# Hybrid encoder trunk on one core: more lead for the filter on VectorE, outer gates of convolution A behind the attention inputs, per-tile staging of the first chunks, five single tiles ahead of doubles in layer 1

## The chip, the cores and the metric

The program runs on one core of a Trainium2 chip. The metric is device time in microseconds (us).

## What is computed

Two layers over a sequence of 2048 positions with 1024 channels, then a final RMSNorm. Cut to what matters:

```
h = rmsnorm(x, norm_g);  proj = h @ w_in           # 1024 -> 3584, 28 tiles of 128 channels
y_a = silu(layernorm(depthwise_conv31(a_u * sigmoid(a_v)) + b)) * silu(a_z)
y_b = b_b * conv3(b_c * b_x) * silu(b_z)
y_c = window_attention(c_q, c_k, c_v, sink) * silu(c_z)      # +-128 positions
y_d = neighbourhood_attention(d_q, d_k, d_v, rpb) * silu(d_z)
x = x + concat(y_a, y_b, y_c, y_d) @ w_out         # 1024 -> 1024, 8 tiles of 128
```

## The kernel before

**Tiles and stages.** The sequence is cut into four chunks of 512 positions. Every fp32 operand of a projection is split in two (hi and lo), and three products are added, so one weight tile of 128 channels on one chunk is 24 matmuls of 512 columns. A job (run, line 859) takes one weight tile over one chunk (a single) or over two chunks (a double, 48 matmuls). The stages are, in order: i00 and i01 (input projection of layer 0, chunks 0 and 1, then 2 and 3), o00 (output projection, chunks 0 and 1), i10, o01, i11, o10, o11. The chunks of a pair sit in slots s0 and s1; an output stage reads its chunk's Y back from DRAM into the same slots (place_y_steps, line 329). In an input stage (in_jobs, line 896) the first RU = 3 tiles run as singles on the first chunk and then on the second, the last RD = 3 likewise, and those between are doubles.

**Weights.** Each half of a weight tile is loaded by SyncE's DMA queue (load_w), cast by ScalarE to whi and subtracted by VectorE to wlo (split_w, line 849). The next job's second half is split after the 24th matmul of a single, twelve matmuls before it is needed.

**The other work.** Attention goes in units (line 628) of 128 queries and two heads: scores s, a softmax on VectorE and ScalarE, transposes pt, products o, and a gate ag; 32 units for each chunk pair, 16 for one chunk, 64 in a layer. They begin once their inputs are marked done (marks, lines 923 and 926). The 31 taps of the depthwise convolution are 31 VectorE instructions for each of two channel tiles and each chunk (tap_steps, line 465). When both channel tiles of a chunk have their taps and the gates az are stored, conv_ln (line 490) runs the LayerNorm and writes Y; it uses POOL for sums, PE for lnm, lnv and rb, and the same two PSUM buffers "s" as the units' scores. Output chunk c waits for its 16 units and for the LayerNorms of chunks c and c+1 (y_ready, line 975).

**What sets the order.** The Python code is a planner that writes out the program order. After every eight matmuls it calls point (line 180), which advances evictions, units and background work and then adds taps. It keeps two clocks of its own: PE by a cost for each matmul (0.228 for one of 512 columns), DVE by 0.12 + 0.00115 per element, never below PE's clock less 1:

```
                clk["dve"] = max(clk["dve"], clk["pe"] - 1.0) + 0.12 + n * 1.15e-3
        while taps and clk["dve"] < clk["pe"] + LEAD:
            tap()
```

These are planning numbers and no times. When built, the framework's scheduler takes the program order as priority and lets an instruction go earlier on its engine where its inputs and buffers are free by its own estimate. In ev_au (line 447) taps are forced out when four filters are queued, and before an odd output chunk of layer 1 the planner waits until no taps are left (line 963). GA = 4 buffers hold gated inputs (gA) and four hold filter sums (accA); TB = 5 buffers "t" serve gates, squares and the LayerNorm.

**The first chunks.** scale_steps multiplies all eight tiles of a chunk by the norm, and then place_steps splits them (lines 296 and 318); chunk 1 goes the same way in second (line 1072). bias_steps (line 761) copies a table for the relative bias into DRAM 128 times (rep, 2256 KB), loads it back and writes the bias tiles; it is called once for each layer.

Of the kernel before, what the change touches and what calls it, by code (L numbers as in the profile page):

```python
# [18 lines left out]
P = 128  # L19
# [36 lines left out]
TB, TH, XTB, GA, GB = 5, 2, 4, 4, 4  # L56
QSB, PRB, PTB = 2, 4, 2
GRP = 8
RU, RD = 3, 3
PF, UNITS, SPACING = 7, 4, 5  # L60
PF_LATE, UNITS_LATE, SPACING_LATE = 3, 6, 2
LEAD = 0.0
KSB, VTB, WB = 3, 3, 3

E_A_U, E_A_V, E_A_Z = 0, 2, 4
# [6 lines left out]
def trunk(ctx, tc, xT, w_in, w_out, par, sink, rpb, fg, trig, cmask, dmask, out):  # L72
# [16 lines left out]
    def T(pool_, shape, dt, tag, bufs, name=None):  # L89
        uid[0] += 1  # L90
        return pool_.tile(shape, dt, tag=tag, bufs=bufs, name=f"{name or tag}_{uid[0]}")
# [78 lines left out]
    evs, bg, units, taps = [], [], [], deque()  # L170
    waiting, done = [], set()
    current, gap, points, begun, turn = [None], [0], [0], [0], [0, 0]
    pace = {"spacing": SPACING, "units": UNITS, "pf": PF}

    def advance(lst):
        for g in list(lst):
# [3 lines left out]
    def point():  # L180
        advance(evs)
        advance(units)
        gap[0] += 1
        points[0] += 1
        if waiting and gap[0] >= pace["spacing"] and len(units) < pace["units"] and begun[0] < turn[0] + QSB:
            group = current[0] or next((w for w in waiting if w[0]()), None)
            if group:
                current[0] = group
                gap[0] = 0
                g = group[1].popleft()()  # L190
                if not group[1]:
                    waiting.remove(group)
                    current[0] = None
                units.append(g)
                next(g)
        advance(bg)
        while taps and clk["dve"] < clk["pe"] + LEAD:
            tap()

    def tap():  # L200
# [24 lines left out]
    def new_slot(s):  # L225
        return (pairs(slot, F32R, f"s{s}h", 4), pairs(slot, F32R, f"s{s}l", 4))
# [25 lines left out]
    def spread(r, n):  # L252
        rb = T(ps, [P, CH], F32, "s", 2, "rb")
        for b in range(0, n, P):
            m = min(P, n - b)
            mm(rb[:, b:b + m], r[:m, b // P:b // P + 1].broadcast_to([m, P]), ident[:m, :m], True, True, 0.12)
        return rb
# [38 lines left out]
    def scale_steps(l, c, xts, per=2):  # L296
        rb = spread(RC[l][:, 4 * c:4 * c + 4], CH)
        yield
        rs = T(gp, [P, CH], F32, "t", TB, "rs")
        act.copy(out=rs, in_=rb)  # L300
        yield
        for k in range(KT):
            dve.scalar_tensor_tensor(out=xts[k], in0=xts[k], scalar=LP[l]["par"][:, PG + k:PG + k + 1], in1=rs,
                                     op0=ALU.mult, op1=ALU.mult)
            if k % per == per - 1:
                yield
        staged[(l, c)] = xts

    def stage_steps(l, c):
        while ("rc", l, c) not in done:  # L310
# [7 lines left out]
    def place_steps(l, c, s):  # L318
        while (l, c) not in staged:
            yield  # L320
        xts = staged.pop((l, c))
        hi, lo = new_slot(s)
        for k in range(KT):
            split(xts[k], hi[k], lo[k])
            if k % 2:
                yield
        acts[(l, c)] = (hi, lo)
# [433 lines left out]
    def bias_steps(l):  # L761
        L = LP[l]
        W = 4 * RPR * RPW
        sp.dma_start(out=L["rep"], in_=rpb[l:l + 1, :].broadcast_to([P, W]))
        yield from hold(4)
        n = 15 * RPW + 32
        Ms = []
        for h in range(4):
            M = T(ap_, [P, 2 * CH], F32, "ks", KSB, "bm") if h < 3 else T(ap_, [P, 2 * CH], F32, "vt", VTB, "bm")
            base = L["rep"][0:1, :]  # L770
            src = bass.AP(tensor=base.tensor, offset=base.offset + h * RPR * RPW + 7 * RPW + 15,
                          ap=[[16 * W - RPW, 8], [W - 1, 16], [1, n]])
            sp.dma_start(out=M[:, :n], in_=src)
            Ms.append(M[:, :16 * RPW].rearrange("p (r c) -> p r c", c=RPW))
        for (o, sz, i, j) in MOFF.values():
            R, rr, C = window(i, j)
            mk = T(ap_, [P, CH], F32, "pth", PTB, "bmk")
            sp.dma_start(out=mk[:, :sz], in_=dmask[:, o:o + sz])
            r0, c0 = ROW_M0[i], COL_M0[j]
            mkv = mk[:, :sz].rearrange("p (g r c) -> p g r c", r=rr, c=C)  # L780
            yield
            yield
            for p in range(2):
                t = T(ap_, [P, 2, CH], F32, "prob", PRB, "bmo")
                for hh in range(2):
                    pool.tensor_tensor(out=t[:, hh, :sz].rearrange("p (g r c) -> p g r c", r=rr, c=C), in0=mkv,  # L786
                                       in1=Ms[2 * p + hh][:, r0:r0 + R, c0:c0 + C].rearrange(
                                           "p (r g) c -> p g r c", r=rr), op=ALU.subtract)
                yield from hold(2)
                sp.dma_start(out=L["bias"][2 * p:2 * p + 2, :, o:o + sz].rearrange("h q n -> q h n"), in_=t[:, :, :sz])  # L790
        done.add(("bias", l))
# [104 lines left out]
    def in_jobs(l, half):  # L896
        A, B = ((0, 1), (2, 3))[half]
        D = [(E_D_K, lambda p: lambda c, pt: ev_dk(l, p, c, pt)),
             (E_D_V, lambda p: lambda c, pt: ev_vd(l, p, c, pt)),
             (E_D_Q, lambda p: lambda c, pt: ev_dq(l, p, c, pt)),  # L900
             (E_D_Z, lambda p: lambda c, pt: ev_z(l, 6 + p, c, pt))]
        lst = [(et + p, ev(p), None) for et, ev in D for p in range(2)]
        C = [(E_C_K, lambda c, pt: ev_rope(l, "k", 0, c, pt), lambda: [load_trig(c) for c in (A, B)]),
             (E_C_V, lambda c, pt: ev_vc(l, c, pt), None),
             (E_C_Q, lambda c, pt: ev_rope(l, "q", 0, c, pt), None),
             (E_C_Q + 1, lambda c, pt: ev_rope(l, "q", 1, c, pt), None),
             (E_C_Z, lambda c, pt: ev_z(l, 4, c, pt), None),
             (E_C_Z + 1, lambda c, pt: ev_z(l, 5, c, pt), None)]
        Aa = []
        for e in range(2):  # L910
            Aa += [(E_A_V + e, lambda c, pt, e=e: ev_av(l, e, c, pt), None),
                   (E_A_U + e, lambda c, pt, e=e: ev_au(l, e, c, pt), None)]
        for e in range(2):
            Aa.append((E_A_Z + e, lambda c, pt, e=e: ev_z(l, e, c, pt), None))
        Bb = []
        for e in range(2):
            Bb += [(E_B_C + e, lambda c, pt, e=e: ev_bc(l, e, c, pt), None),
                   (E_B_X + e, lambda c, pt, e=e: ev_bx(l, e, c, pt), None),
                   (E_B_Z + e, lambda c, pt, e=e: ev_bz(l, e, c, pt), None),
                   (E_B_B + e, lambda c, pt, e=e: ev_bb(l, e, c, pt), None)]  # L920
        if half == 0:
            order = lst + C + Aa + Bb
            marks = {7: ("qd", l, 0), 13: ("qc", l, 0), 19: [("az", l, 0), ("az", l, 1)]}
        else:
            order = Aa + lst + C + Bb
            marks = {5: [("az", l, 2), ("az", l, 3)], 13: ("qd", l, 1), 19: ("qc", l, 1)}

        def mark(i):
            ks = marks[i] if isinstance(marks[i], list) else [marks[i]]

            def late():
                yield from hold(8)
                for k in ks:
                    done.add(k)
            bg.append(late())

        N = len(order)

        def emit(i, keys, last):
            et, ev, pre = order[i]  # L940
            job(wtile(l, et), keys, ev, pre if keys[0][-1] == A or len(keys) == 2 else None,
                (lambda: mark(i)) if last and i in marks else None)

        for i in range(RU):
            emit(i, [(l, A)], False)
        for i in range(RU):
            emit(i, [(l, B)], True)
        for i in range(RU, N - RD):
            emit(i, [(l, A), (l, B)], True)
        for i in range(N - RD, N):  # L950
            emit(i, [(l, A)], False)
        first = len(jobs) - 1
        for i in range(N - RD, N):
            emit(i, [(l, B)], True)
        return first, len(jobs) - 1
# [73 lines left out]
    then(o10[1], y_place(1, 3, 1))  # L1029

    def late():
        pace.update(spacing=SPACING_LATE, units=UNITS_LATE, pf=PF_LATE)
        return
        yield

# [28 lines left out]
            pass  # L1064
    for hf in range(2):
        split_w(jobs[0], hf)
    for _ in scale_steps(0, 0, x0):
        pass
    for _ in place_steps(0, 0, 0):
        pass  # L1070

    def second():
        yield from stat_steps(1, x1)
        yield from scale_steps(0, 1, x1)
        yield from place_steps(0, 1, 1)

    def consts():
        yield from hold(3)
# [98 lines left out]
```

## Time and profile before

| | us |
|---|---|
| median of 3 runs (2089.1 to 2099.12) | 2096.69 |
| the profiled execution | 2092.12 |
| its span, first to last instruction | 2090.3 |
| PE busy in the span | 1967.2 |
| VectorE (DVE) busy | 1553.1 |
| ScalarE (ACT) busy | 1040.1 |

The profile shows one execution. Matmul ends are modelled and overlap, so PE's pace is read from starts: two starts of a steady stretch tell how long one matmul holds the engine. A window row gives busy time, granted clock (1.00 is 2.4 GHz, 0.50 is 1.2 GHz) and DMA share of a stretch.

### The profile page before, as it was taken

Reading aid. Unit: us, or ns where it says so; the run is one execution under the profiler, and the core shown is the slowest. Engines: PE = TensorE matmul, PEld = TensorE weight load, DVE = VectorE, ACT = ScalarE, POOL = GpSimd, SP = SyncE. Lnnn points to the kernel's source line nnn. Section 1 sums busy time; section 2 is a strip of 40 time slices with the busy share of each in tenths; the row PEclk is TensorE's granted clock in tenths of the full one; section 3 lists DMA queues with packets and bytes.
Section 4 is the critical chain, followed back from the end, with each engine's and each line's share of the span. In section 5 each row is a group of like instructions: output and inputs, shape, how many; then the busy total and the mean of one; then the engine's idle time right before and its main releaser. Section 6 shows DMA issues by size and latency. Waiting matters only on the chain.

```text
span 2090.3 us, 29475 instructions
## 1 busy us (share of the span) xinstructions
PE 1967.2 (94%) x9436; PEld 1638.5 (78%) x9436; DVE 1553.1 (74%) x3531; ACT 1040.1 (50%) x2217; POOL 181.6 (9%) x158
## 2 busy tenths in 40 slices
PE   5899999999999999899999999989999899996697
PEld 4778888787888878788888888878888788885585
DVE  6734799968985677776659998755995567866855
ACT  4435434523355466566654446532237566665542
POOL 0610000071010000000100000001000000100100
PEclk9999999999999999999999999999999999998698
DMA  9985533576455479867653467863638866577353
GB/s 281 305 280 175 150 121 92 170 257 200 151 172 171 158 246 305 242 201 236 183 164 119 143 179 220 244 197 105 179 132 252 227 193 207 154 221 221 120 177 115
DMA packets 233850, 400.65 MB, mean 192 GB/s; under 512 B 26848, under 2 KB 92000, under 8 KB 233440
## 3 DMA queue, kind: packets, MB, share of 16 engines
q1 hardware_dynamic: 233696, 398.77, 62.2%
q8 instruction: 75, 1.23, 0.3%
q14 instruction: 79, 0.65, 0.1%
HBM read 297.68 MB, written 105.61 MB: 193 GB/s over the span
## 4 chain that ended last, share of the span: by engine, by line
PE 71%; DMA 14%; DVE 9%; ACT 2%; issue 2%; SPq 1%; POOL 1%; DVEq 0%; POOLq 0%; ACTq 0%
PE mm L135 59%; PE o L135 3%; PE s L135 3%; PE pt L716 3%; DMA prob<-bias 2%; DMA wraw<-in_w_in_dram 2%; DVE wlo L128 1%; DMA s1l<-Y 1%; DVE xt L128 1%; DMA qs<-QD 1%; DMA qs<-QC 1%; DMA wraw<-in_w_out_dram 1%; POOL bmo L786 1%; DMA Y<-accA 1%; DVE accA L128 1%
## 5 line engine op out<-in xcount | busy, mean ns | idle before, releaser
L135 PE MATMUL mm<-s1h,whi 128*128 128x512 f32 x1152 | 458.8, 399 | 22.5 <-ACT s1h L218 10.8
L218 ACT CAST whi<-wraw 128x512 fp32r<-128x512 f32 x400 | 246.6, 618 | 444.9 <-PE mm L135 348.9
L135 PE MATMUL mm<-s1l,whi 128*128 128x512 f32 x1152 | 457.8, 398 | 6.2 <-DVE s1l L128 6.2
L135 PE MATMUL mm<-s0h,whi 128*128 128x512 f32 x1152 | 455.4, 396 | 7.0 <-ACT s0h L218 5.3
L135 PE MATMUL mm<-s0l,whi 128*128 128x512 f32 x1152 | 454.4, 395 | 4.9 <-DVE s0l L128 4.9
L135 PE MATMUL mm<-s1h,wlo 128*128 128x512 f32 x1152 | 455.2, 397 | 4.0 <-DVE wlo L128 4.0
L135 PE MATMUL mm<-s0h,wlo 128*128 128x512 f32 x1152 | 455.3, 396 | 1.0 <-DVE wlo L128 0.7
L128 DVE TENSOR_TENSOR wlo<-wraw,whi 128x512 fp32r<-128x512 f32 x400 | 289.3, 725 | 159.7 <-ACT whi L218 142.4
L128 DVE SCALAR_TENSOR_TENSOR accA<-gA,par,accA 128x512 f32<-128x512 f32 (+1 forms) x480 | 352.8, 774 | 0.6
L135 PEld LDWEIGHTS mm<-s1h,whi 128*128 128x128 f32 x1152 | 219.6, 191 | 69.8 <-ACT s1h L218 12.1
L135 PEld LDWEIGHTS mm<-s1l,whi 128*128 128x128 f32 x1152 | 219.9, 191 | 51.0 <-DVE s1l L128 7.5
L135 PEld LDWEIGHTS mm<-s0h,whi 128*128 128x128 f32 x1152 | 218.2, 190 | 51.5 <-ACT s0h L218 5.7
L135 PEld LDWEIGHTS mm<-s1h,wlo 128*128 128x128 f32 x1152 | 219.7, 191 | 49.4 <-DVE wlo L128 5.9
L135 PEld LDWEIGHTS mm<-s0l,whi 128*128 128x128 f32 x1152 | 218.2, 189 | 50.2 <-DVE s0l L128 6.3
L135 PEld LDWEIGHTS mm<-s0h,wlo 128*128 128x128 f32 x1152 | 218.2, 189 | 45.5 <-DVE wlo L128 3.2
L689 ACT ACTIVATE prob<-prob,mn 128x384 f32<-128x384 f32 (+4 forms) x256 | 155.3, 607 | 116.1 <-DVE mn L128 115.0
L706 ACT ACTIVATE prob<-prob,sm 128x384 f32<-128x384 f32 (+4 forms) x256 | 142.2, 602 | 49.8 <-DVE sm L128 43.9
L128 DVE TENSOR_TENSOR pth<-pt,pth 128x512 fp32r<-128x512 f32 (+3 forms) x248 | 138.5, 573 | 32.6 <-ACT pth L218 31.6
L135 PE MATMUL s<-ks,qs 128*128 128x384 f32 (+4 forms) x512 | 129.6, 357 | 21.1 <-DMA qs<-QC 7.0
L218 ACT CAST pth<-pt 128x512 fp32r<-128x512 f32 (+3 forms) x248 | 115.0, 495 | 66.6 <-PE pt L716 46.1
L135 PE MATMUL o<-pth,vt 128*128 128x256 f32 (+2 forms) x784 | 129.6, 297 | 8.2 <-DVE oy L128 5.2
L135 PEld LDWEIGHTS o<-pth,vt 128*128 128x128 f32 (+2 forms) x784 | 117.4, 199 | 20.7 <-issue 4.1
(120 smaller groups left out, 2039.5 us busy)
## 6 DMA issues: line engine op xcount, KB each, us to landing
wraw<-in_w_in_dram SPq DMA_DIRECT2D x272, 256.0 KB
wraw<-in_w_out_dram SPq DMA_DIRECT2D x128, 256.0 KB
qs<-QD SPq DMA_DIRECT2D x128, 128.0 KB
qs<-QC SPq DMA_DIRECT2D x128, 128.0 KB
G<-g SPq DMA_DIRECT2D x48, 256.0 KB
vt<-VD SPq DMA_DIRECT2D x144, 72.0 KB
xt<-in_xT_dram SPq DMA_DIRECT2D x20, 512.0 KB
KD<-t SPq DMA_DIRECT2D x32, 256.0 KB
```

What stands on the lines that cost most here:

```text
L128: return fn(*a, **kw)
L135: pe.matmul(out=out, lhsT=lhsT, rhs=rhs, start=start, stop=stop)
L218: act.copy(out=hi, in_=src)
L689: act.activation(out=t[:, hh, :n], in_=t[:, hh, :n], func=AF.Exp, bias=mn[:, hh:hh + 1], scale=-1.0, accum_out=sm[:, hh:hh + 1])
L706: act.activation(out=t[:, hh, :n], in_=t[:, hh, :n], func=AF.Copy, scale=sm[:, hh:hh + 1])
L716: pe.transpose(out=tp[:kw, b_, hh, :], in_=t[:, hh, kb * kw:(kb + 1) * kw], identity=ident)
L786: pool.tensor_tensor(out=t[:, hh, :sz].rearrange("p (g r c) -> p g r c", r=rr, c=C), in0=mkv, in1=Ms[2 * p + hh][:, r0:r0 + R, c0:c0 + C]. ...
```

## The change

LEAD becomes 6.0 in both layers, so taps are written out until the DVE clock is 6 ahead of PE's. In the second input stage of each layer the order was: six tiles of convolution A, attention inputs D and C, then B; now the four tiles u and v of A come first, then D and C, then the two gates az, then B; the marks follow. In layer 1 the first five tiles are singles in place of three. The first two chunks are scaled and split tile by tile. The copy rep is tied behind the DMA that was written just before it.

```diff
-RU, RD = 3, 3
+RU, RU1, RD = 3, 5, 3
-LEAD = 0.0
+LEAD, LEAD_LATE = 6.0, 6.0
...
-        while taps and clk["dve"] < clk["pe"] + LEAD:
+        while taps and clk["dve"] < clk["pe"] + pace["lead"]:
             tap()
...
+    def scale_place_steps(l, c, xts, s):
+        rb = spread(RC[l][:, 4 * c:4 * c + 4], CH)
+        yield
+        rs = T(gp, [P, CH], F32, "t", TB, "rs")
+        act.copy(out=rs, in_=rb)
+        yield
+        hi, lo = new_slot(s)
+        for k in range(KT):
+            dve.scalar_tensor_tensor(out=xts[k], in0=xts[k], scalar=LP[l]["par"][:, PG + k:PG + k + 1], in1=rs,
+                                     op0=ALU.mult, op1=ALU.mult)
+            split(xts[k], hi[k], lo[k])
+            if k % 2:
+                yield
+        acts[(l, c)] = (hi, lo)
...
-        sp.dma_start(out=L["rep"], in_=rpb[l:l + 1, :].broadcast_to([P, W]))
+        tc.keep_in_program_order(sp.dma_start(out=L["rep"], in_=rpb[l:l + 1, :].broadcast_to([P, W])))
...
-            order = Aa + lst + C + Bb
-            marks = {5: [("az", l, 2), ("az", l, 3)], 13: ("qd", l, 1), 19: ("qc", l, 1)}
+            order = Aa[:4] + lst + C + Aa[4:] + Bb
+            marks = {11: ("qd", l, 1), 17: ("qc", l, 1), 19: [("az", l, 2), ("az", l, 3)]}
...
-        for i in range(RU):
+        ru = RU1 if l else RU
+        for i in range(ru):
             emit(i, [(l, A)], False)
-        for i in range(RU):
+        for i in range(ru):
             emit(i, [(l, B)], True)
-        for i in range(RU, N - RD):
+        for i in range(ru, N - RD):
...
-    for _ in scale_steps(0, 0, x0):
-        pass
-    for _ in place_steps(0, 0, 0):
+    for _ in scale_place_steps(0, 0, x0, 0):
         pass
     def second():
         yield from stat_steps(1, x1)
-        yield from scale_steps(0, 1, x1)
-        yield from place_steps(0, 1, 1)
+        yield from scale_place_steps(0, 1, x1, 1)
```

## Rows read from the trace of the kernel before

**Rows 1.** Windows: stretch, length, busy PE, PEld, DVE, ACT, POOL (xcount), clock, DMA, GB/s.

```profile
0.00:60.00 60.00, 26.92 (x109) 21.76 (x109) 37.16 (x87) 24.72 (x43) 0.70 (x6) 0.94 0.93 279
60.00:150.00 90.00, 86.89 (x382) 71.25 (x382) 51.35 (x79) 33.79 (x61) 39.16 (x36) 0.97 0.94 313
...
1450.00:1600.00 150.00, 150.00 (x695) 124.89 (x694) 134.33 (x230) 61.87 (x115) 11.04 (x7) 1.00 0.55 168
...
1899.00:1976.00 77.00, 46.39 (x214) 38.46 (x213) 57.34 (x204) 43.50 (x111) 4.54 (x5) 0.68 0.49 145
```

**Rows 2.** Windows of the projection matmuls mm alone, same columns without POOL.

```profile
1899.00:1976.00 77.00, 0.03 (x1) 0.03 (x1) 0.67 (x1) 0.00 (x0) 0.68 0.49 145
1976.00:2072.00 96.00, 92.69 (x384) 74.50 (x384) 10.30 (x15) 0.00 (x0) 0.96 0.52 170
```

**Rows 3.** Timeline of PE at full pace: start, length, instruction.

```profile
1889.66 0.39 PE L135 MATMUL mm<-s1h,wlo 128*128 128x512 f32 x1
1889.89 0.39 PE L135 MATMUL mm<-s1h,whi 128*128 128x512 f32 x1
```

**Rows 4.** Chain that ended last, 1854 to 2010: start, length, what.

```profile
1853.65 0.53 PE s L135 x4
1854.17 0.66 PE pt L716 x6
1854.83 0.72 PE o L135 x6
...
1989.45 6.69 DMA Y<-accA
...
1998.09 8.91 DMA s1l<-Y
```

**Rows 5.** Timeline of POOL: first two sums of the LayerNorm of layer 1, chunk 3.

```profile
1823.38 1.76 POOL L493 TENSOR_TENSOR lns<-accA,accA 128x512 f32<-128x512 f32 x1
1948.19 1.27 POOL L507 TENSOR_TENSOR lns<-lns,lns 128x512 f32<-128x512 f32 x1 [123.06 <-ACT lns L505]
```

**Rows 6.** Timeline of DVE: taps, a weight split between them, the last gate.

```profile
1539.38 4.79 DVE L128 SCALAR_TENSOR_TENSOR accA<-gA,par,accA 128x527 f32<-128x527 f32 x7
1544.52 0.69 DVE L128 TENSOR_TENSOR wlo<-wraw,whi 128x512 fp32r<-128x512 f32 x1 [0.35 <-ACT whi L218]
...
1566.65 0.76 DVE L128 SCALAR_TENSOR_TENSOR accA<-gA,par,accA 128x527 f32<-128x527 f32 x1
...
1970.31 0.27 DVE L128 SCALAR_TENSOR_TENSOR ag<-oy,ag 128x128 f32<-128x128 f32 x1
```

**Rows 7.** Timeline of SyncE's DMA queue: issue, queue time, transfer.

```profile
1824.43 0.38 SPq L539 DMA_DIRECT2D Y<-accA  x1
1829.06 1.86 SPq L332 DMA_DIRECT2D s1l<-Y  x3
...
1964.80 3.64 SPq L539 DMA_DIRECT2D Y<-accA  x2
1970.62 0.56 SPq L332 DMA_DIRECT2D s0l<-Y  x1
```

**Rows 8.** Timeline of PE at the start of i11's second chunk [idle before].

```profile
1402.41 0.79 PE L135 MATMUL mm<-s1l,whi 128*128 128x512 f32 x1 [3.57 <-DVE s1l L128]
```

**Rows 9.** Chain in the first 75 us: start, length, what.

```profile
20.48 19.99 DMA wraw<-in_w_in_dram
...
42.72 15.65 DMA wraw<-in_w_in_dram
```

**Rows 10.** Timeline of SyncE's DMA queue: the two table copies.

```profile
16.80 0.62 SPq L764 DMA_DIRECT2D rep<-in_rpb_dram  x1
...
19.79 0.60 SPq L764 DMA_DIRECT2D rep<-in_rpb_dram  x1
```

**Rows 11.** Timeline of DVE: scaling of chunk 1.

```profile
47.63 5.39 DVE L128 SCALAR_TENSOR_TENSOR prob<-prob,par,rs 128x512 f32<-128x512 f32 x8 [2.65 <-ACT rs L300]
```

**Rows 12.** PE's longest wait in the first 150 us.

```profile
PE mm L135 <- ACT s1h L218: 10.8, 1, 10.8
```

More of the change, by code (lines that the diff above doesn't have):

```diff
@@ L172, in trunk @@
     current, gap, points, begun, turn = [None], [0], [0], [0], [0, 0]
-    pace = {"spacing": SPACING, "units": UNITS, "pf": PF}
+    pace = {"spacing": SPACING, "units": UNITS, "pf": PF, "lead": LEAD}
     def advance(lst):
@@ L1031, in late @@
     def late():
-        pace.update(spacing=SPACING_LATE, units=UNITS_LATE, pf=PF_LATE)
+        pace.update(spacing=SPACING_LATE, units=UNITS_LATE, pf=PF_LATE, lead=LEAD_LATE)
         return
```

## The prediction

> **What bounds the kernel now.** I read the windows by stage first. From 1450 to 1600 PE is busy all the time, and 1967 us of the whole span of 2090; a projection matmul of 512 columns starts every 0.227 us (1889.66, then 1889.89) [rows 1, 3]. Where PE is that full, work moved about inside a stage is worth nothing. What can be won is idle PE, and there are two large pieces: the first 60 us, where PE is busy for 27, and the stretch from 1899 to 1976, where it is busy for 46 of 77 us at a granted clock of 0.68 and runs no projection matmul but one [rows 1, 2].
>
> The second piece is the more important, so I ask what ended it. Output chunk 2 (o11) starts at 1976, after its Y has been loaded to s0l at 1970.62, and that load follows the LayerNorm's stores Y<-accA at 1964.80 [rows 7]. So stage o11 waits for the LayerNorm of convolution A, chunk 3. Yet the last tap of that convolution ended at 1567 [rows 6]. The LayerNorm's first sum stands on POOL at 1823 and its second only at 1948, 123 us later [rows 5]. No engine needs that long: the steps stand late in the program order. The planner writes the taps out only while its DVE clock is behind PE's, and beside attention it hardly ever is; the scheduler pulls the taps themselves forward, since their inputs are there, but the LayerNorm is written after the last tap, behind the attention units, and its PSUM tile comes from the two buffers that the units' scores take in turn. So the place of the last tap in the program, not its execution, sets the end. The gate's last write of attention is at 1970.31 [rows 6], just as late: removing one of the two is not enough, and the change has to move both.
>
> **LEAD = 6, and the order in the second input stages.** By the planner's own costs a double job is 48 x 0.228 = 10.94, and its two weight splits and two evictions take 4 x 0.709 = 2.84 of DVE. At LEAD 0 the DVE clock falls up to 0.8 below the floor between two points 1.82 apart, and that room is forgotten. At LEAD 6 it never falls there, so a double takes (10.94 - 2.84)/0.709 = 11 taps. The 124 taps of half 1 in layer 1 then fit into about eleven doubles or their equal in singles, and five singles on each chunk and seven doubles pass before attention begins. Does the real DVE follow? Seven taps take 4.79 us back to back, 0.684 each against a planned 0.709 to 0.726, and DVE was busy 134 of 150 us in the stretch that held most of these taps [rows 6, 1]. It does. The LayerNorm is then held by the later of the taps and az, whose gates now come as tiles 19 and 20 of 28, the places that Cz0 and Cz1 had; behind them come eight double tiles and sixteen output jobs of 24 matmuls, 768 x 0.227 = 174 us, before o10 ends at 1899. So this Y is complete in time.
>
> The attention inputs come two doubles earlier: 2 x 48 x 0.227 = 21.8 us [rows 3]. Also no units are written in a block ahead of output chunk 1 any more, since the wait for the taps finds none; they interleave with its eight jobs. I expect the last unit to end beside o11's first chunk, and o11's second chunk to find its input.
>
> The price: in the 77 us window PE's own work, at full pace, is about 12 units (7 whose 28 score matmuls fall in it, some 5 still open) of 0.53 + 0.66 + 0.72 = 1.91 us [rows 4], 23 us, and some 4 for sums and the LayerNorm: 27. So 50 us are idle or lost to the low clock. The next 96 us hold 384 matmuls, 87 us at full pace [rows 2, 3], and about 3 us of sums: 6 more, from the low clock and waits for splits after the gap. Together **-56**. Against it I set **+4** for waits on loads that PE sees when attention runs beside o11, as it does in o10.
>
> **Output chunk 1 of layer 1.** Its load s1l is issued at 1829.06 behind Y<-accA of chunk 2's LayerNorm at 1824.43 [rows 7]; with that LayerNorm early the load needs only attention, which is then ahead. The load's way is about 10 us, in part under attention work: **-6**, between 0 and -9.
>
> **Five singles in layer 1.** The second chunk's first single comes two singles, 2 x 24 x 0.227 = 10.9 us, later [rows 3]. In i11 PE waits 3.57 us for s1l there and then runs at the pace of the splits [rows 8]; that goes under cover: **-5**, between 0 and -7. It costs two more weight tiles in each half, four in all, each with two loads of 256 KB, two casts and two subtractions of 0.69 us [rows 6], beside 48 matmuls that PE runs anyway: **+1**, between 0 and +4, since singles give the second split only 12 x 0.227 = 2.7 us before it is needed.
>
> **The first chunks.** The two copies of rep are issued at 16.80 and 19.79 [rows 10], 2256 KB each. The weight load issued at 20.48 needs 20 us and the next, at 42.72, 15.65 us [rows 9], with the DMA engines at 0.93 and 279 GB/s [rows 1]; 4.5 MB at that rate are 16 us. Now layer 1's copy leaves the start for good, and layer 0's stands behind the stores and loads written before it. PE's wait of 10.8 us for s1h [rows 12] ends with that weight; what is late next is chunk 1 itself, scaled from 47.63 to 53.02 [rows 11]. With scaling and split tile by tile its first s1h is there after one tile instead of eight, so the wait is covered but for about 2 us. Chunk 0 keeps its end, as DVE does the same sixteen instructions. Against that, layer 0's copy and its reload now fall into 60 to 150, where the DMA engines are at 0.94 [rows 1], and a queue that waits for the copy to land holds the weights behind it. **-8**, between -14 and +5. The bias tiles come later, but the first unit that reads them is far behind.
>
> **What is added elsewhere.** The moved gates az and the LayerNorms of chunks 2 and 3 now run together beside the B tiles, and share five buffers "t" with them; an eviction that waits for one holds a PSUM tile and so PE. No row shows this: below, nothing can be gained; above, one LayerNorm's load and sum, about as long as Y<-accA plus s1l, 15 us [rows 4]. I take **+3**, near zero, since POOL and DVE have room there. The lead itself can put taps ahead of a weight split: 6 planned units are nine taps, 9 x 0.684 = 6.2 us, against 2.7 us of slack in a single; 3.5 us once for each stretch that starts to fill with taps, four of them, so 0 to +14, and I take **+3**, as DVE runs faster than planned. In layer 0 the earlier attention relieves o00 a little: **-2**, 0 to -5.
>
> Sum: -56 + 4 - 6 - 5 + 1 - 8 + 3 + 3 - 2 = -66. The profiled execution took 2092.1 us, 0.2% below the median of the runs, so I expect 2026 for one like it and 2031 beside the median; I say **2028**.
>
> **A rule against it.** The rows show a weight split standing 0.35 us for its cast while taps stand before and after it [rows 6]. The Trainium skill, Perfetto Trace Analysis, section Tensor Engine Instruction, says that ACT, DVE and GPSIMD are strict FIFO, while PE can pull weight loads ahead. The row agrees as far as it goes. By that rule no split passes a tap that was placed before it, and with the +14 above instead of +3 the sum would be 2039.
>
> **The rivals.** *Attention alone holds the end* (0.10). The last gate write stays at 1970 because units depend on their own chain of loads, softmax and transposes, not on when they start. Then o11's first chunk runs early, and its second starts after a store and a load, 1970 + 6.7 + 8.9 + 1.2 for the split = 1987 [rows 4, 6], instead of 1976 + 8 x 24 x 0.227 + the 6 us above = 2026. That is -39, with -3 from the start and the singles after their costs, and beside the median: **2055**. For it: units and LayerNorm end together now. Against it: PE has matmuls in every stretch before, and the units are written two doubles earlier. *The change does not do what it says* (0.06): if the taps still are not all written when attention fills DVE, the LayerNorm stays last, and only the start and the singles gain what the added waits cost: **2090**. Against it: at eleven taps a double nearly all are out when attention begins, and a remainder of twenty still has the C tiles' room. *VectorE becomes the bound* (0.07): if the lead holds again and again, every single with taps queued pays 3.5 us. In layer 1 those are the last six of i10, the sixteen of o01 and ten of i11, 32 x 3.5 = 112 us, against -66: **2140**. It decides when DVE needs more per tap than the planner charges, 0.709; at 0.684 it falls short of that point.
>
> **How the numbers follow.** The forecast holds with 0.77, in its own range of 2003 to 2055 (2028 less 25 with the start and the added waits at their good ends and the loads hidden; plus 27 with the added waits and the weight tiles at their bad ends). The range of the whole runs from 1998, five below that for stages that gain what I set at nothing, to 2078, past the first rival; it leaves out the last two rivals. A run of this kernel can tell half a per cent, 10 us, from no change. Faster takes the forecast and the first rival, 0.87; same the second, 0.06; slower the third, 0.07.
>
> **What would show it.** In the profile after: PE busy over 90% in the last 130 us before its final matmul, at a clock near 1.00; the LayerNorm's sums of chunk 3 on POOL before o10 starts; s0l loaded for o11 while o10 runs; no rep in SyncE's first 40 us and weight loads of under 10 us there. It is wrong if PE idles before o11's second chunk (first rival), if the LayerNorm of chunk 3 still follows the last unit (second), or if PE waits for wlo by tens of us (third).

## The result, and the profile after

The changed kernel takes 2058.9 us against 2095.4 before (medians of four runs), a ratio of 0.9831 with a 95% interval of [0.9802, 0.9861]: 37 us won, of 66 forecast. That is clear of noise, and 1.7% where 3.1% were forecast. The profiled execution has a span of 2058.4 us, against 2090.3. These two spans differ by 32 us and not by 37, since the profiled execution of before was 3 us faster than its median, and that of after 1 us slower.

Windows by stage of the changed kernel (stretch, length, busy PE, PEld, DVE, ACT, POOL, clock, DMA share, GB/s): the start, i01, a stretch of i11, and o11.

```profile
0.00:60.00 60.00, 33.24 (x126) 26.53 (x127) 44.22 (x98) 29.23 (x52) 1.47 (x7) 0.94 0.77 251
60.00:150.00 90.00, 85.79 (x382) 70.11 (x381) 44.55 (x70) 32.87 (x57) 35.80 (x37) 0.98 0.92 307
388.80:769.30 380.50, 364.33 (x1725) 302.84 (x1724) 297.16 (x618) 170.02 (x341) 75.32 (x65) 0.98 0.62 191
...
1590.00:1670.00 80.00, 67.12 (x329) 55.05 (x328) 37.04 (x103) 39.06 (x88) 2.61 (x2) 0.96 0.75 217
...
1920.90:2040.60 119.70, 109.78 (x518) 90.25 (x516) 86.79 (x202) 51.80 (x104) 0.00 (x0) 0.94 0.51 169
```

The start answers to [rows 1]: PE is busy for 33 of the first 60 us instead of 27, and the two stretches together hold 5.2 us more PE work. Stage i01, on which the prediction spent little, has 16 us without PE. In 1590 to 1670 PE is idle for 13 of 80 us.

The LayerNorm of layer 1, chunk 3 on POOL, and its stores with the loads of Y behind them on SyncE's DMA queue, changed kernel:

```profile
1660.99 1.32 POOL L508 TENSOR_TENSOR lns<-accA,accA 128x512 f32<-128x512 f32 x1 [2.58 <-DMA G<-g]
...
1718.06 1.30 POOL L522 TENSOR_TENSOR lns<-lns,lns 128x512 f32<-128x512 f32 x1 [1.67 <-ACT lns L520]
```

```profile
1825.99 0.33 SPq L554 DMA_DIRECT2D Y<-accA  x1
1851.21 0.56 SPq L347 DMA_DIRECT2D s0l<-Y  x1
```

```profile
1993.84 0.38 SPq L766 DMA_DIRECT2D Y<-ag  x1
1997.02 1.21 SPq L347 DMA_DIRECT2D s1l<-Y  x2
```

The last gate write of attention on VectorE, changed kernel:

```profile
1993.31 0.28 DVE L128 SCALAR_TENSOR_TENSOR ag<-oy,ag 128x128 f32<-128x128 f32 x1
```

Against [rows 5] the sums come 162 and 230 us earlier, and s0l, loaded at 1970 before [rows 7], is loaded while o10 runs. The hole ahead of output chunk 2 is gone. But the last load of Y now waits for attention, whose last gate write at 1993.31 is later than the 1970.31 of before [rows 6], and output chunk 3, the second of o11, waits for it. Two more of the forecast's signs: from 1910 to 2041 PE is busy for 121 of 131 us (92%) at a clock of 0.95, and the first copy rep is issued at 41.37 us, just behind the 40 that were asked.

To see where the rest went, I add up by stage the time that PE spends over its full pace: for every instruction of PE the time to the start of the next one, less the lower quartile of that time for the same form in the trace of before (0.227 us for a projection matmul). So work that moves from one stage to another doesn't show as a loss. The stages begin at their first projection matmul.

```
us over full pace   i00   i01   o00   i10   o01   i11   o10   o11
before             33.2  11.7  15.9  17.4  12.6  23.3  67.4   7.2
after              28.9  30.7  12.7  10.1  12.6  35.2   9.1  18.2
e1_no_lead         28.8  26.0   6.5  10.8  11.3  24.4  55.2   7.9
e2_rep1_free       29.4  17.8  16.7  10.8  10.7  36.5   8.3  17.4
e3_old_order       28.2  32.6  20.3  13.8  18.2  17.6   9.8  38.2
e4_lead_late       33.0  29.0   8.0  10.4  11.2  34.0   8.3  20.7
e5_old_staging     31.0  29.2   9.6  10.5  14.0  32.7   7.1  17.3
e6_ru3             28.2  29.1   9.4  14.3  14.0  39.9   8.2  18.5
e7_no_pins         34.7  18.7  16.2   9.7  13.4  35.1   5.6  17.3
e8_bias_early      27.6  30.9  13.7  10.0  15.4  15.8  11.1  25.2
e10_mark9          30.0  30.0  18.0   9.2  18.5  38.5   6.3   2.7
e9_all             29.5  22.3  18.0   9.4  18.7  23.0  13.7  16.8
e11_rep_bias       31.9  18.1  15.1  10.9   9.5  15.3  12.6  26.3
e12_rep_bias_late  29.7  15.0  12.2  10.3  10.3  15.8  12.4  17.6
```

The edit of each run stands in the next section. e1 and e4 share everything up to the end of i10, and differ there by up to 4 us a stage (28.8 and 33.0 in i00): single entries tell nothing below that. The stages of after gain 47 us in o10 and o11, 4 in i00, 3 in o00 and 7 in i10, and lose 19 in i01 and 12 in i11: -31, as the spans say (-32).

### The profile page after: what moved, and what is told of

Its sections match the earlier page's. It is cut to its first block, busy times and chain, and to the rows that moved or that the text cites. A ratio compares the mean times of both kernels' runs of the same rounds, so it can differ in the third digit from the quotient of the medians.

```text
span 2058.4 us, 29509 instructions
## 1 busy us (share of the span) xinstructions
PE 1949.5 (95%) x9436; PEld 1625.4 (79%) x9436; DVE 1555.1 (76%) x3539; ACT 1045.1 (51%) x2225; POOL 182.5 (9%) x158
## 4 chain that ended last, share of the span: by engine, by line
PE 74%; DMA 11%; DVE 7%; issue 2%; ACT 2%; SPq 2%; POOL 1%; DVEq 0%; ACTq 0%; POOLq 0%
PE mm L135 62%; PE o L135 4%; PE s L135 4%; PE pt L731 3%; DMA prob<-bias 2%; DMA rep<-in_rpb_dram 1%; DVE wlo L128 1%; DVE accA L128 1%; DMA wraw<-in_w_out_dram 1%; DMA s1l<-Y 1%; DMA VD<-hv 1%; DMA bm<-rep 1%; PE rb L135 1%; DMA X<-xo 1%; POOL bmo L801 1%
## 5 line engine op out<-in xcount | busy, mean ns | idle before, releaser
L218 ACT CAST whi<-wraw 128x512 fp32r<-128x512 f32 x408 | 251.8, 618 | 452.6 <-PE mm L135 341.5
L128 DVE TENSOR_TENSOR wlo<-wraw,whi 128x512 fp32r<-128x512 f32 x408 | 293.6, 720 | 135.6 <-ACT whi L218 118.3
L135 PE MATMUL s<-ks,qs 128*128 128x384 f32 (+4 forms) x512 | 128.4, 352 | 15.5 <-DVE mn L128 12.7
L135 PE MATMUL o<-pth,vt 128*128 128x256 f32 (+2 forms) x784 | 123.5, 289 | 3.3 <-ACT whi L218 2.4
L731 PE MATMUL pt<-ident,prob 128*128 128x128 f32 (+2 forms) x784 | 115.7, 274 | 10.2 <-DVE pth L128 10.2
```

What stands on the lines that cost most here:

```text
L128: return fn(*a, **kw)
L135: pe.matmul(out=out, lhsT=lhsT, rhs=rhs, start=start, stop=stop)
L218: act.copy(out=hi, in_=src)
L731: pe.transpose(out=tp[:kw, b_, hh, :], in_=t[:, hh, kb * kw:(kb + 1) * kw], identity=ident)
```

## The experiments

**Lead and order.** Each is taken back alone.

```diff
-LEAD, LEAD_LATE = 6.0, 6.0
+LEAD, LEAD_LATE = 0.0, 0.0
```

> The changed kernel with LEAD and LEAD_LATE at 0; tile order, staging, pins and five singles stay. Theory (the place of the last tap in the program set the end): the taps of layer 1, half 1 are again written out among the attention units, LayerNorm's first POOL sum of chunk 3 comes after 1780 us instead of 1661, and PE idles ahead of output chunk 2 as it did before; about 30 of the 47 us that o10 and o11 gained go back, and the 13 us that the early LayerNorms of layer 0 cost beside the bias work come back as a gain: 2065 to 2085 us. Rival (the order of the tiles alone made the gain): 2040 to 2055 us, LayerNorm of chunk 3 done before o10 ends.

```diff
-            order = Aa[:4] + lst + C + Aa[4:] + Bb
-            marks = {11: ("qd", l, 1), 17: ("qc", l, 1), 19: [("az", l, 2), ("az", l, 3)]}
+            order = Aa + lst + C + Bb
+            marks = {5: [("az", l, 2), ("az", l, 3)], 13: ("qd", l, 1), 19: ("qc", l, 1)}
```

> The changed kernel with the second input stages in the old order (all six tiles of convolution A first, marks as before); the lead and the rest stay. Theory of the prediction (both the LayerNorm and attention must come earlier): the inputs of attention come two double tiles, about 22 us, later; the last gate write, 1993.6 us in the changed kernel, goes to about 2010, and PE waits in front of o11's second chunk instead of 4.9 us for about 20: 2070 to 2085 us. Rival (the lead alone does it, units catch up at six in flight): within 6 us of the changed kernel, 2053 to 2065 us.

Without the lead 2077.3 us, 0.9914 [0.9883, 0.9945]; with the old order 2085.5, 0.9945 [0.9924, 0.9966], at the upper end of its expectation. The LayerNorm sums of chunk 3 on POOL, without the lead:

```profile
1811.30 1.31 POOL L508 TENSOR_TENSOR lns<-accA,accA 128x512 f32<-128x512 f32 x1 [39.12 <-DVE sm L128]
1928.26 1.27 POOL L522 TENSOR_TENSOR lns<-lns,lns 128x512 f32<-128x512 f32 x1 [115.65 <-ACT lns L520]
```

The last stores and loads of Y on SyncE's queue, old order:

```profile
2014.75 0.32 SPq L766 DMA_DIRECT2D Y<-ag  x1
2016.76 1.21 SPq L347 DMA_DIRECT2D s1l<-Y  x2
```

Without the lead the LayerNorm is late again and o10 loses 55 us over full pace. With the lead and the old order it is early, but attention's last store goes from 1993.84 to 2014.75, and o11 loses 38, though not in one wait of 20 us as expected (the longest are 6.1 us for mn and 4.5 for s1h). So the tap's place in the program and the time at which attention starts both set the end: by the ratios the change without its order is worth 0.6%, without its lead 0.9%, and whole 1.7%. One number of the first expectation missed: i01 gave back 5 us without the lead, not 13, so the early LayerNorms were not what i01 suffered from in the main.

**The copy of layer 1's table.** PE's two longest waits in 430 to 530 of the changed kernel (waiting <- what it waited for: us, times, longest), POOL there, and the chain:

```profile
PE lnv L135 <- POOL lns L522: 6.3, 1, 6.3
PE rb L135 <- DVE rl L128: 6.2, 1, 6.2
```

```profile
440.98 0.76 POOL L801 TENSOR_TENSOR bmo<-bmk,bm 128x288 f32<-128x288 f32 x1 [10.28 <-DMA bm<-rep]
...
456.83 6.28 POOL L801 TENSOR_TENSOR bmo<-bmk,bm 128x288 f32<-128x288 f32 x8 [4.34 <-DMA bmk<-in_dmask_dram]
463.06 1.23 POOL L551 TENSOR_TENSOR accA<-accA,ga 128x497 f32<-128x497 f32 x1
464.25 1.26 POOL L522 TENSOR_TENSOR lns<-lns,lns 128x512 f32<-128x512 f32 x1
465.47 4.65 POOL L801 TENSOR_TENSOR bmo<-bmk,bm 128x512 f32<-128x512 f32 x4
470.07 1.25 POOL L551 TENSOR_TENSOR accA<-accA,ga 128x497 f32<-128x497 f32 x1
```

```profile
422.45 12.98 DMA rep<-in_rpb_dram
...
436.85 8.10 DMA bm<-rep
```

The squares that the sum at 464.25 reads were finished on ACT at 449.70:

```profile
449.07 0.63 ACT L520 ACTIVATE lns<-accA 128x512 f32<-128x512 f32 x1
```

The sum stood 14.6 us behind bias subtractions, which waited for loads of their own, and PE stood 6.3 us for it. The gate products at 463.06 and 470.07 stood there too; they held accA buffers, and the next tap waited 17 us for one:

```profile
471.31 3.75 DVE L128 TENSOR_SCALAR accA<-gA,par 128x512 f32<-128x512 f32 x1 [17.07 <-POOL accA L551]
```

After it the taps and the small steps of the LayerNorm's reciprocal root (rn, rl) took turns on VectorE, which is the second wait of 6.2 us. The Trainium skill, Perfetto Trace Analysis, section Tensor Engine Instruction, calls GPSIMD strict FIFO; these rows agree.

```diff
-        tc.keep_in_program_order(sp.dma_start(out=L["rep"], in_=rpb[l:l + 1, :].broadcast_to([P, W])))
+        ld = sp.dma_start(out=L["rep"], in_=rpb[l:l + 1, :].broadcast_to([P, W]))
+        if l == 0:
+            tc.keep_in_program_order(ld)
```

> The changed kernel, with the copy of layer 1's bias table (rep) no longer kept in program order; layer 0's stays kept. Theory (the D tiles of i01 lost about 15 us because that copy, issued at 422 us, lands late, POOL holds bias subtractions that wait for it, and the LayerNorm sums stand behind them in POOL's queue): stage i01 goes from 380 us to 362 to 368 us; the copy is back in the first 40 us and costs 3 to 8 us there; in all 2043 to 2055 us. Rival (the early LayerNorms of layer 0, which the lead makes, collide with the bias work wherever its table comes from): i01 stays at 375 us or more, and with the copy back at the start the time is 2059 to 2068 us.

2049.9 us, 0.9779 [0.9758, 0.9800], an interval below that of the changed kernel. All of PE's waits in 389 to 530 with layer 1's copy free:

```profile
PE rb L135 <- DVE rl L128: 1.4, 1, 1.4
PE mm L135 <- ACT t L373: 1.2, 1, 1.2
PE mm L135 <- ACT th L439: 1.0, 1, 1.0
PE mm L135 <- ACT whi L218: 0.5, 1, 0.5
```

i01 takes 367.7 us, 17.8 over full pace, and i00 stays where it was, 29.4, so the 3 to 8 us expected there did not come. The next run asks whether the lead had moved the LayerNorms into that place.

```diff
-LEAD, LEAD_LATE = 6.0, 6.0
+LEAD, LEAD_LATE = 0.0, 6.0
```

> The changed kernel with LEAD at 0 and LEAD_LATE still at 6: the lead works in layer 1's second half only. It tells what moved the LayerNorms of layer 0 into the late bias work. If the lead is the cause of the loss in i01, i01 goes from 380 us to 360 to 367 us and the whole to 2042 to 2050 us. If the late copy of the bias table is the cause by itself, i01 stays at 373 us or more and the whole at 2053 to 2063 us.

LEAD_LATE takes over at the end of i10, so this run has no lead in layer 0 and in i10. 2053.6 us, 0.9784 [0.9753, 0.9815]. i01 stays at 29.0: the late copy is cause enough. The total is lower by 5 us all the same, but the interval overlaps that of after. In o00 this run and e1, both without the lead, have 8.0 and 6.5 over full pace, and after has 12.7, at the edge of what single entries tell.

**The first chunks.** One run has the old staging with both copies kept in program order, the other the new staging with neither.

```diff
-    for _ in scale_place_steps(0, 0, x0, 0):
+    for _ in scale_steps(0, 0, x0):
+        pass
+    for _ in place_steps(0, 0, 0):
...
-        yield from scale_place_steps(0, 1, x1, 1)
+        yield from scale_steps(0, 1, x1)
+        yield from place_steps(0, 1, 1)
```

> The changed kernel with the old staging of the first two chunks (all eight tiles scaled, then all eight split). Stage i00 takes 367.1 us in the changed kernel against 371.3 before. If the tile-by-tile staging made this gain, i00 goes to 371 us or more, PE waits about 10 us again in front of the first s1h, and the whole is 2063 to 2067 us. If the gain came from the copies of rep that left the start, i00 stays within 1.5 us of 367 and the whole at 2057 to 2061 us.

```diff
-        tc.keep_in_program_order(sp.dma_start(out=L["rep"], in_=rpb[l:l + 1, :].broadcast_to([P, W])))
+        sp.dma_start(out=L["rep"], in_=rpb[l:l + 1, :].broadcast_to([P, W]))
```

> The changed kernel with neither copy of rep kept in program order; staging by tile, lead, order and five singles stay. Both copies should be issued before 25 us again. With layer 1's copy alone set free the time was 2049.9 us and i00 did not change. Theory of the prediction (copies at the start hold the weights there): i00 goes from 367 to 371 us or more, 2053 to 2058 us in all. Rival (the start has room for both copies, tile-by-tile staging made the whole gain): i00 at 365 to 369 us and 2047 to 2052 us.

2055.1 us, 0.9816 [0.9786, 0.9846], and 2052.1, 0.9792 [0.9759, 0.9824]; neither total can be told from that of after. The first lies below both of its expectations, the second between its two. i00 took 369.2 us with the old staging, between its two expectations, and 372.9 with both copies free, as the theory had it. PE's wait for s1h in the first 150 us, [rows 12], in the changed kernel, then with the old staging, then with both copies free:

```profile
PE mm L135 <- ACT s1h L218: 1.4, 1, 1.4
```

```profile
PE mm L135 <- ACT s1h L218: 1.4, 1, 1.4
```

```profile
PE mm L135 <- ACT s1h L218: 13.5, 1, 13.5
```

The wait falls with the copies, not with the staging. With both free the chain holds a weight load of 18 us at 42 again, as [rows 9] did:

```profile
42.23 18.23 DMA wraw<-in_w_in_dram
```

Why the staging doesn't matter there, VectorE and ScalarE with the old staging show (first two lines); the third is ScalarE before the change:

```profile
46.59 5.39 DVE L128 SCALAR_TENSOR_TENSOR prob<-prob,par,rs 128x512 f32<-128x512 f32 x8 [0.39 <-ACT rs L300]
48.51 0.61 ACT L218 CAST s1h<-prob 128x512 fp32r<-128x512 f32 x1
...
58.44 0.62 ACT L218 CAST whi<-wraw 128x512 fp32r<-128x512 f32 x1 [5.04 <-DMA wraw<-in_w_in_dram]
```

The first s1h is a cast on ScalarE that needs only its own tile. It ran at 48.51, while VectorE was scaling the eight tiles until 51.98. Before the change the cast of s1h at 58.97 came behind this cast of a weight, which had waited for its load. The old-staging run does not hold all else fixed: layer 0's copy is issued at 55.1 there instead of 41.4, and one later wait of PE, for an eviction at 105 us, is 7.6 us instead of 3.3. A few us from the staging are not excluded.

One copy at the start leaves the wait for s1h at 1.4 us (e2, i00 at 29.4), two bring it back (e7, i00 at 34.7, as 33.2 before).

**Five singles.**

```diff
-RU, RU1, RD = 3, 5, 3
+RU, RU1, RD = 3, 3, 3
```

> The changed kernel with three instead of five single tiles ahead of the doubles in layer 1. Forecast: PE waits again for s1l in i11 and runs at the pace of the splits after it, 5 us, while two weight tiles in each half are saved, 1 us: 2061 to 2066 us. Rival (the second chunk's splits are out in time by now, since nothing stands in their way): 2056 to 2060 us.

2073.1 us, 0.9883 [0.9853, 0.9913], from runs of 2064 to 2077, above both expectations. PE's wait in 1385 to 1460 is the one of [rows 8] again:

```profile
PE mm L135 <- DVE s1l L128: 4.2, 1, 4.2
```

The profiled execution lost 4.7 us in i11, as forecast, and its span is 4 us longer; the timed runs lost more, and no view here says where.

**The loads of late attention units.** VectorE's wait for bias tiles in 1590 to 1670, changed kernel (first fence), and with the loads two points earlier (second), with the window of the latter:

```diff
-PF_LATE, UNITS_LATE, SPACING_LATE = 3, 6, 2
+PF_LATE, UNITS_LATE, SPACING_LATE = 5, 6, 2
...
-            yield from hold(pace["pf"] - 3)
+            b0_ = 3 if pace["pf"] == PF else PF_LATE
+            yield from hold(pace["pf"] - b0_)
...
-            yield from hold(3)
+            yield from hold(b0_)
```

> The changed kernel with the bias tile of an attention unit of layer 1's late pace loaded five points instead of three ahead of its scores (PF_LATE 5, the load right after that of the queries). In the changed kernel VectorE waits 28 us for these loads between 1590 and 1670 us and PE 9.6 us behind it. If the lateness of the load is what i11 lost (35 us over full pace against 23 before), VectorE's wait there falls below 12 us, i11 gets 5 to 10 us shorter, and the whole is 2047 to 2055 us. If the DMA engines are what is short there, or the buffers come free too late, the loads land no earlier: 2056 to 2063 us, with VectorE's wait above 20 us.

```profile
DVE prob L128 <- DMA prob<-bias: 28.2, 8, 5.5
```

```profile
DVE prob L128 <- DMA prob<-bias: 3.2, 3, 1.4
```

```profile
1590.00:1670.00 80.00, 77.15 (x394) 65.46 (x393) 43.83 (x124) 48.87 (x109) 2.61 (x2) 0.96 0.86 250
```

2054.4 us, 0.9805 [0.9779, 0.9830]; the interval overlaps that of after, and the stages tell more than the total. PE is busy 77 of 80 us instead of 67, with the DMA engines at 0.86 instead of 0.75, so they were not what was short: the loads were issued too late. i11 goes from 35.2 to 15.8 over full pace. PE felt it as a wait for mn, which VectorE writes right behind the softmax step that reads the bias tile. That wait in i11, before the change and in the changed kernel:

```profile
PE s L135 <- DVE mn L128: 0.9, 1, 0.9
```

```profile
PE s L135 <- DVE mn L128: 9.6, 5, 3.7
```

With the early loads no wait for mn is left in i11. Of the 19 us some 12 come back elsewhere: o11 loses 7 more, since attention ends there later (5.5 units have their scores in o11, against 2), and o01 and o10 together 5, within the scatter.

**Attention's end.**

```diff
-            marks = {11: ("qd", l, 1), 17: ("qc", l, 1), 19: [("az", l, 2), ("az", l, 3)]}
+            marks = {9: ("qd", l, 1), 15: ("qc", l, 1), 19: [("az", l, 2), ("az", l, 3)]}
```

> The changed kernel with the attention units of the second halves allowed to begin two double tiles earlier, ahead of the gate tiles Dz and Cz instead of behind them. It asks whether the end of attention still costs PE time in o11 (18.2 us over full pace; 7.2 before). If so, the last gate write comes before 1985 us, PE no longer waits 4.9 us for s1h in o11, and the whole is 2045 to 2054 us. Rival (units are paced by their own loads and move nothing at the end): o11 within 3 us of 119.7 and the whole at 2055 to 2064 us.

2056.3 us, 0.9803 [0.9775, 0.9832]. Both expectations failed in part. The last gate write comes at 1968.84 and o11 runs near full pace (2.7 over it), so the 15 us of o11 were attention's:

```profile
1968.84 0.28 DVE L128 SCALAR_TENSOR_TENSOR ag<-oy,ag 128x128 f32<-128x128 f32 x1
```

But o00 and o01 lose 5 and 6 us more and i11 3, and the total stays: the earlier marks hold in both layers.

**Together.** First the free copy with the early loads, then these with the earlier units, then the first two with the lead only from the end of i10 on.

> The changed kernel with layer 1's rep copy free again and the bias tiles of late attention units loaded five points ahead. Alone the two gave 9 us and 4 us against the changed kernel. If the costs stand in different stages (i01 and i11) they add up: 2042 to 2049 us, i01 at 365 to 370 us and i11 at 384 to 390 us. If the end of attention holds the rest, the second gain is handed back in o11 (131 us with the bias loaded early against 120): 2048 to 2053 us.

> All three together: layer 1's rep copy free, bias tiles of late units five points ahead, attention of the second halves two double tiles earlier. If each cost is a place of its own: 2058.9 less 9, less 4 to 10, less 5: 2033 to 2044 us. If the third does not reach the end of attention: as with the first two alone, 2042 to 2053 us.

> The changed kernel with layer 1's rep copy free, the bias tiles of late attention units five points ahead, and LEAD at 0 until the late pace begins (LEAD_LATE stays 6). With the first two the time was 2042.2 us; the lead taken out of layer 0 alone gave 5 us, and o00 went from 121.8 to 117.9 us. If taps put ahead of weight splits and evictions in layer 0 are what the lead costs there, o00 again gets 4 to 8 us shorter than the 124.2 us of that kernel and the whole is 2033 to 2040 us. If that difference was scatter between runs, or the late LayerNorms of layer 0 cost as much in i01 or o00, the whole is 2040 to 2047 us.

2042.2 us, 0.9736 [0.9708, 0.9764]: the two add up, with i01 (368 us) and i11 (385 us) where they were expected. With the earlier units 2054.9, 0.9795 [0.9762, 0.9828]: outside both expectations and worse than without them, so that piece is dropped. The last version takes 2025.0 us, 0.9656 [0.9627, 0.9685], and beats both kernels. Its windows of i01, i11, o10 and o11:

```profile
389.50:750.80 361.30, 355.86 (x1693) 295.68 (x1692) 282.79 (x567) 161.80 (x326) 66.27 (x56) 1.00 0.58 184
1365.70:1754.30 388.60, 383.01 (x1900) 320.45 (x1900) 315.66 (x722) 211.76 (x442) 37.25 (x26) 1.00 0.65 195
1754.30:1882.90 128.60, 122.91 (x630) 102.59 (x629) 98.25 (x264) 87.26 (x206) 2.82 (x3) 0.99 0.73 219
1882.90:2005.40 122.50, 111.92 (x545) 92.54 (x543) 88.02 (x219) 58.02 (x125) 0.00 (x0) 0.96 0.53 171
```

The lead taken out of layer 0 and i10 gave 17 us here, more than the 2 to 9 expected and more than the 5 of e4. i00, i01 and o00 give 8 of them, each within the scatter (o00 3, not 4 to 8), and o11 gives 9. Its last gate write comes 76 us after o11's start instead of 85, though nothing of layer 1's late pace was changed. Why is open.

## Why the prediction was half right

The mechanism held for the hole, and the sign with it; the size did not. 2058.9 lies just above the forecast's own range of 2003 to 2055, inside the range of the whole, and near the 2055 of the first rival. That nearness is chance: the losses stand in i01 and i11, which that rival does not name. Its second chunk of o11 starts at 1987, and the measured one at 1986.5, but PE did not stand idle until then: it waited 5 us in the 66 us of the first chunk, which also held the scores of two units and the ends of others. In the range, the bad ends that the prediction names add up to 26 and not 27, which changes nothing. The sizes, by the prediction's steps:

- **The hole, -56, with -6 for output chunk 1 and +4 beside o11**: -58 forecast, -47 measured (o10 and o11). The hole in o10 closed in full. The +4 was too small: o11 lost 11 us more than before. PE's waits in o11 name attention; the first two of the changed kernel are:

```profile
PE mm L135 <- ACT s1h L218: 4.6, 1, 4.6
PE pt L731 <- DVE pth L128: 4.2, 2, 4.0
```

  That is a part of the first rival, which let attention hold the end and o11's second chunk pay for it. Its gate write was to stay near 1970; it came even later, at 1993.

- **Attention in full stages**: this is a term the sum didn't have. I priced waits on loads only beside o11. The change moves units from the hole, where a wait of PE cost nothing since PE was idle, into i11 (31 units' scores instead of 25), where every one costs. i11 lost 12 us, about 16 if the gain of the singles is left out. PE's wait for mn went from 0.9 to 9.6 us there, and e8, which loads the bias tiles earlier, removes it and wins 19 us: these loads were issued too late.

- **The copy of layer 1's table**: the sum gave it nothing, for it "leaves the start for good". I asked what the start gains and priced the new place of layer 0's copy, not that of layer 1's. It landed at 435, with the reload behind it, in front of the LayerNorm on POOL: 13 of the 19 us that i01 lost (e2: 30.7 to 17.8; e7: 18.7). The other 6 are not separated.

- **The first chunks, -8**: -4 measured in i00, within the scatter of 4. The prediction gave two reasons, the copies and the scaling by tile, and the second failed. The wait of 10.8 us went with the copies, and e5 has it at 1.4 with the old staging too, since the cast of s1h never waited for eight tiles. Of the 9.4 us won there 3.3 came back as a wait for s1l. The cost foreseen for layer 0's copy shows in the chain of after (first two lines) and in SyncE's queue (the others): behind the weight loads of 44.36 the next one is issued only at 69.52.

```profile
41.37 12.39 DMA rep<-in_rpb_dram
...
55.20 8.71 DMA bm<-rep
```

```profile
44.36 2.87 SPq L862 DMA_DIRECT2D wraw<-in_w_in_dram  x2
...
69.52 0.36 SPq L862 DMA_DIRECT2D wraw<-in_w_in_dram  x1
```

- **Five singles, -5 and +1**: right in the profile (4.7 us in i11, with the wait of 4.2 us back), and the timed runs put it higher.

- **LayerNorms and az on five buffers, +3**: PE's list of waits in i11 names none of them; so it comes to nothing that shows. **Lead ahead of weight splits, +3**: PE's waits for whi and wlo in the whole execution are 8.1 and 4.9 us, against 7.2 and 4.8 before, so the term comes to about 1, and the +14 did not come. But the lead costs something that the sum does not have: taken out of layer 0 and i10 it gave 5 us (e4) and 17 us (e12). By what way is not shown. **Layer 0, -2**: o00 gave 3, and 8 without the lead (e4).

- **i10** gained 7 us that the sum set at nothing. Four units fewer stand in it; no run separates this.

*The change does not do what it says* fell with the LayerNorm at 1718. *VectorE becomes the bound* fell too, by the same waits for whi and wlo.

## What to carry to other kernels

A hole in the bounding engine also hides the waits of all work that stands in it: when the work is moved into full stages, each of its waits has a price, so list the waits of that work beside the size of the hole. An instruction kept in program order lands somewhere else: ask for each copy what is queued there, on every engine that consumes it. And where a gain has several parts, try the parts in separate stages: here the lead paid in the second half of layer 1, and the last version, without it ahead of that, was 17 us faster than the same with it.

## What the runs showed that I had not expected

One copy of the table (2256 KB) at the start left PE's wait for s1h at 1.4 us (e2, as in after), two made it 13.5 (e7), and i00 lost some 6 us, just above the scatter; I had taken the cost as proportional to the bytes. And the stretch from 1590 to 1670, with the DMA engines at 0.75, moved more when its loads were issued two points earlier, 250 GB/s against 217: a share of 0.75 was lateness, not the engines' limit.
